# An encoder on one core: the first products in plain float32, a projection ahead of its norm's sums, and GpSimd's splits from a later point

## The chip, the cores and the metric

The kernel runs on one core of a Trainium2 chip. The time is device microseconds of one execution; three executions of the kernel before took 1354.34, 1357.28 and 1357.43 us, so their median is 1357.28 us. The engines are TensorE (PE, with its weight loads shown apart as PEld), VectorE (DVE), ScalarE (ACT), GpSimd (POOL) and SyncE (SP, which here only issues DMAs).

## The reference, cut to what matters

Input is x (1, 256, 1024) in float32, with 16 learned meta tokens prepended, so 272 tokens in all. Two layers (DEPTH = 2) run over them:

```python
def rms_norm(x, g):
    xf = x.astype(jnp.float32)
    y = xf * lax.rsqrt(jnp.mean(xf * xf, axis=-1, keepdims=True) + EPS)
    return (y * g.astype(jnp.float32)).astype(x.dtype)

def swiglu(h, w_in, w_out):
    gate, up = jnp.split(h @ w_in, 2, axis=-1)
    return (jax.nn.silu(gate) * up) @ w_out

for l in range(DEPTH):
    h = h + 0.5 * swiglu(rms_norm(h, ffn1_norm[l]), ffn1_w_in[l], ffn1_w_out[l])
    h = h + hybrid_mixer(rms_norm(h, mix_norm[l]), w_in[l], ...)
    h = h + 0.5 * swiglu(rms_norm(h, ffn2_norm[l]), ffn2_w_in[l], ffn2_w_out[l])
return rms_norm(h, final_norm)[:, META:]
```

The hidden width of the SwiGLU is 2816. The mixer makes one combined projection (q, k, v of three attentions A, B and C, and gates), runs the three attentions, multiplies each by its own output weights and its gate, adds them, and applies w_out. All inputs are float32.

## The kernel before, in words

**Layout and products.** Activations lie transposed in SBUF: `h` holds 1024 features as 8 slices of 128 partitions, each with 272 tokens (256 grid tokens, then 16 meta tokens). Every weight product is made of three TensorE products. A float32 weight block arrives by DMA as `raw` (128 x 1024, 512 KB, a "unit" of four 128-row slices and 256 columns). ACT rounds it to `hi` (L227, type float32r), and DVE or POOL writes the rest, `lo` = raw - hi (L228). The activation is split in the same way into `xh` and `xl`. `mm` then adds xh·hi, xl·hi and xh·lo in PSUM (L271, L272, L273), for each of 8 slices k and each of 2 output halves m: 48 TensorE products of 272 tokens for a 1024-deep group of 256 outputs. `raw` has 4 buffers, `hi` and `lo` have 4 each, and the PSUM tile `acc` has 2.

**The norm.** A `Norm` object keeps x' = g·h, without the factor 1/rms, as `xh` and `xl`; `pair(j)` makes two of the 8 slices (xh by DVE at L312 for the odd slice and by ACT at L314 for the even one, xl by DVE at L315), squares h on ACT (L318), and adds the squares up into `ss` (L321, on POOL, for the last pair on DVE). `finish` sums over the partitions by two plain float32 products with a matrix of ones (L326), and makes rstd `r` = 1/rms with one square root on ACT (L291, which first loads an activation table) and six DVE instructions (L329, L292 to L296). The results of the products are multiplied by r afterwards, as they leave PSUM.

**The start.** x comes in as two tiles of 128 tokens; `load_pair(j)` transposes two slices on TensorE (L191) into one PSUM bank, and ACT (L194) and DVE (L195) copy them into `h`. `norm.pair` follows. `first` holds the `hi` and `lo` of the first gate group of the first SwiGLU, and `ffn` makes its 48 products, then `finish`, then the 48 products of the first up group.

**The mixer.** `mixer` calls `norm.finish` and then makes its projections, B's values first (`B_V`, two groups of 256 outputs), then B's keys and queries, A's, C's and the gates, woven into the attentions. Each result of the first four groups is multiplied by r while it leaves PSUM (L700, L704). While `in_mixer[0]` is set, `lo_engine` gives each third unit's `lo` to POOL, by a counter that runs over all plain units of the program; the others are DVE's.

**What sets the order.** The instructions of each engine are put in their order when the kernel is built, by a scheduler that may move independent ones past each other; on the chip every engine runs its own list in order. All weight DMAs are issued by SP, in order.

Of the kernel before, what the change touches and what calls it, by code (L numbers as in the profile page):

```python
# [10 lines left out]
F32 = mybir.dt.float32  # L11
F32R = mybir.dt.float32r
AF = mybir.ActivationFunctionType
# [78 lines left out]
def encoder_kernel(ctx: ExitStack, tc: tile.TileContext, x, meta_tokens, ffn1_norm, ffn1_w_in, ffn1_w_out,  # L92
# [20 lines left out]
    def scr():  # L113
        return sb.tile([128, 2, T], F32, name=nm("scr"), tag="scr", bufs=5)

    def acc_tile():
        return ps.tile([128, 2, 512], F32, name=nm("acc"), tag="acc", bufs=2)
# [4 lines left out]
    def bc(ap, n):  # L122
        return ap[:, None, :].to_broadcast([ap.shape[0], n, ap.shape[1]])
# [61 lines left out]
    def load_pair(j):  # L185

        pt = bank("s", 3)
        for i in range(2):
            for k in range(2):
                c0 = (2 * j + k) * 128  # L190
                PE.transpose(pt[:, (2 * i + k) * 128:(2 * i + k + 1) * 128], x_nat[i][:, c0:c0 + 128], ident)  # L191
        hv = h[:, 2 * j:2 * j + 2, :GRID].rearrange("p k (c r) -> p k r c", r=ROWS)
        pv = pt.rearrange("p (i k r c) -> p i k r c", i=2, k=2, r=2)
        ACT.copy(hv[:, :, 0:2, :], pv[:, 0])  # L194
        DVE.tensor_copy(hv[:, :, 2:4, :], pv[:, 1])  # L195

    gshuf = const.tile([128, 4], F32, name="gshuf")
    swap16 = [(i + 16) % 32 for i in range(32)]
# [61 lines left out]
    def mm(acc, units, xh, xl, xk, n):  # L260

        rows = [(hi, lo, kk) for hi, lo in units for kk in range(hi.shape[1])]
        for k, (hi, lo, kk) in enumerate(rows):
            if isinstance(xh, list):
                rh, rl = xh[k // 4][:, k % 4, :n], xl[k // 4][:, k % 4, :n]
            else:
                rh, rl = xh[:, xk + k, :n], xl[:, xk + k, :n]
            for m in range(2):
                o = acc[:, m, :n]
                a, b = hi[:, kk, m * 128:(m + 1) * 128], lo[:, kk, m * 128:(m + 1) * 128]  # L270
                PE.matmul(o, a, rh, start=k == 0, stop=False)  # L271
                PE.matmul(o, a, rl, start=False, stop=False)  # L272
                PE.matmul(o, b, rh, start=False, stop=k == len(rows) - 1)  # L273
# [24 lines left out]
    class Norm:  # L298
# [5 lines left out]
            self.xl = big.tile([128, 8, T], F32R, name=nm("xl"), tag="xl")  # L304
            self.ss = big.tile([128, 2, T], F32, name=nm("ss"), tag="ss")

        def pair(self, j, n):

            for k in (2 * j + 1, 2 * j):
                g = gcol[:, self.g0 + k:self.g0 + k + 1]  # L310
                if k % 2:
                    DVE.tensor_scalar(self.xh[:, k, :n], h[:, k, :n], g, None, op0=ALU.mult)  # L312
                else:
                    ACT.activation(self.xh[:, k, :n], h[:, k, :n], AF.Copy, scale=g)  # L314
                DVE.scalar_tensor_tensor(self.xl[:, k, :n], h[:, k, :n], g, self.xh[:, k, :n].bitcast(F32),  # L315
                                         op0=ALU.mult, op1=ALU.subtract)
            dst = (scr() if j else self.ss)[:, :, :n]
            ACT.activation(dst, h[:, 2 * j:2 * j + 2, :n], AF.Square)  # L318
            if j:
                ss = self.ss[:, :, :n]  # L320
                (DVE if j == 3 else POOL).tensor_tensor(ss, ss, dst, op=ALU.add)  # L321
# [25 lines left out]
    def ffn(w1, w2, norm, nxt, n, first=None):  # L347
        r = rb = None
        for half, (k0, nk) in enumerate(((0, 12), (12, 10))):
            hh = big.tile([128, 12, T], F32R, name=nm("hh"), tag="hh")  # L350
            hl = big.tile([128, 12, T], F32R, name=nm("hl"), tag="hl")
            for j in range(nk // 2):
                ga = acc_tile()
                mm(ga, (r is None and first) or plain(w1, 0, 8, (k0 + 2 * j) * 128), norm.xh, norm.xl, 0, n)
                if r is None:
                    r = norm.finish(n)
                    rb = bc(r[:, :n], 2)
                ua = acc_tile()
                mm(ua, plain(w1, 0, 8, DFF + (k0 + 2 * j) * 128), norm.xh, norm.xl, 0, n)
                g = scr()[:, :, :n]  # L360
                gate, up = ga[:, :, :n], ua[:, :, :n]
                if half == 0 and j == 0:
                    u = scr()[:, :, :n]
                    ACT.copy(g, gate)
                    ACT.copy(u, up)
                    gate, up = g, u
                DVE.tensor_tensor(g, gate, rb, op=ALU.mult)  # L367
                ACT.activation(g, g, AF.Silu)
                DVE.tensor_tensor(g, g, rb, op=ALU.mult)
                DVE.tensor_tensor(g, up, g, op=ALU.mult)  # L370
                split(hh[:, 2 * j:2 * j + 2, :n], hl[:, 2 * j:2 * j + 2, :n], g)
            if first and not half:
                other_gains()
            for mp in range(4):
                residual(mp, plain(w2, k0 * 128, nk, mp * 256), hh, hl, n, nxt if half else None)
# [291 lines left out]
    def mixer(l, norm, nxt, last):  # L667
# [3 lines left out]
            late_dma(cst[:, n_id:], consts[:, n_id:])  # L671
            late_dma(sink, sink_a.partition_broadcast(128))
        biases = [bias_load(l, qi) for qi in range(2)]
        r = norm.finish(T)
        rb = bc(r, 2)
        xh, xl = norm.xh, norm.xl
        oh = big.tile([128, 12, T], F32R, name=nm("oh"), tag="hh")
        ol = big.tile([128, 12, T], F32R, name=nm("ol"), tag="hl")
# [6 lines left out]
        def q_tile():  # L685
            return qk(4, T)
# [4 lines left out]

        vb, kb = qk(4, 2, KB), qk(4, 2, KB)
        qb = q_tile()
        for dst, c0 in ((vb, B_V), (kb, B_K)):
            for half in range(2):
                a = proj(plain(w, 0, 8, c0 + half * 256))
                for qi in range(2):
                    t0 = qi * 96
                    for m in range(2):
                        DVE.tensor_tensor(  # L700
                            dst[:, 2 * half + m, qi, :160].rearrange("p (r c) -> p r c", r=4),
                            a[:, m, t0:t0 + 160].rearrange("p (c r) -> p r c", r=4),
                            r[:, t0:t0 + 160].rearrange("p (c r) -> p r c", r=4), op=ALU.mult)
                    DVE.tensor_tensor(dst[:, 2 * half:2 * half + 2, qi, 160:], a[:, :, GRID:T],  # L704
                                      bc(r[:, GRID:], 2), op=ALU.mult)
# [158 lines left out]
    class Final:  # L864
# [24 lines left out]
        def finish(self):  # L889
# [9 lines left out]
            for qi in range(2):  # L899
# [2 lines left out]
                ACT.activation(self.y[qi][:, 512:], self.pt[qi], AF.Copy, scale=rc)  # L902
                (nc.sync if qi == 0 else ACT).dma_start(dst[qi], self.y[qi])

    norm = Norm(0)
    load_pair(0)
    norm.pair(0, T)
    first = plain(ffn1_w_in[0], 0, 8, 0)
    for j in range(1, 4):
        load_pair(j)  # L910
        norm.pair(j, T)
    for l in range(DEPTH):
        last = l == DEPTH - 1
        nxt = Norm(16 + 8 * l)
        ffn(ffn1_w_in[l], ffn1_w_out[l], norm, nxt, T, first if l == 0 else None)
        norm, nxt = nxt, Norm(32 + 8 * l)
        in_mixer[0] = True
        mixer(l, norm, nxt, last)
        in_mixer[0] = False
        norm, nxt = nxt, (Final() if last else Norm(8))  # L920
        ffn(ffn2_w_in[l], ffn2_w_out[l], norm, nxt, GRID if last else T)
        norm = nxt
# [28 lines left out]
```

## Time and profile before

| | before |
|---|---|
| runs | 1354.34, 1357.28, 1357.43 us |
| profiled execution | 1356.25 us |
| its span, first to last instruction | 1354.5 us |
| PE busy | 1330.5 us (98%) |
| DVE busy | 888.4 us (66%) |
| ACT busy | 649.2 us (48%) |
| POOL busy | 164.7 us (12%) |
| mean granted TensorE clock | 0.991 of full |

The profile is of one execution. "Busy" is the time in which an engine had an instruction; the ends of TensorE's products are modelled and overlap, so their spacing is read from their starts. A row of the timeline gives the start, the duration, the engine, the line of the kernel, the operation, `out<-in` by the names in the program, the shape, the count, and in brackets how long the engine had been idle before it and what ended that. A plain float32 product shows as two records, a float32r product as one. Line numbers are those of the kernel before; in the changed kernel the lines from L199 on have moved (L271 to L273 are L278 to L280 there, L326 is L337, L228 is L235, L312 is L319, L315 is L322, L321 is L332).

### The profile page before, as it was taken

How to read it: one execution, taken by the hardware profiler on the slowest of the kernel's cores; microseconds unless marked ns; L12 is line 12 of the kernel's file. 1: busy time of each engine (PE TensorE's matmuls, PEld its weight loads, DVE VectorE, ACT ScalarE, POOL GpSimd, SP SyncE). 2: the span in 40 equal slices, each digit the busy share in tenths (PEclk: the TensorE clock that was granted, in tenths of full speed). 3: DMA queues.
4: the chain of work that ended last, by engine and by line, in shares of the span. 5: the costliest groups of instructions: out<-in, count | busy, mean ns of one | idle time of the engine just before them, and what ended most of it. 6: DMA issues, size and time to landing. Idle time of an engine off the chain costs nothing.

```text
span 1354.5 us, 25919 instructions
## 1 busy us (share of the span) xinstructions
PE 1330.5 (98%) x10699; PEld 1290.3 (95%) x10699; DVE 888.4 (66%) x1319; ACT 649.2 (48%) x933; POOL 164.7 (12%) x99
## 2 busy tenths in 40 slices
PE   8999999999999999999999999999999999999997
PEld 7999999988898999999999999999889899999997
DVE  7655668588555587646676556676876556865663
ACT  6443444466454455434455434445555545544444
POOL 1000002332122210000000000022322233000000
PEclk9999999999999999999999999999989999999998
DMA  7765556432334566555565555454324456665652
GB/s 218 203 184 176 181 177 188 141 109 89 115 110 125 176 195 187 184 172 173 162 187 180 171 175 182 158 172 149 101 86 118 133 154 192 192 188 187 187 172 78
DMA packets 239010, 217.52 MB, mean 161 GB/s; under 512 B 24804, under 2 KB 237980, under 8 KB 238764
## 3 DMA queue, kind: packets, MB, share of 16 engines
q1 hardware_dynamic: 238540, 215.20, 52.0%
q8 instruction: 84, 1.38, 0.4%
q10 hardware_dynamic: 352, 0.66, 0.1%
q14 instruction: 34, 0.28, 0.1%
HBM read 214.78 MB, written 1.05 MB: 159 GB/s over the span
## 4 chain that ended last, share of the span: by engine, by line
PE 92%; DVE 5%; ACT 1%; issue 1%; DMA 0%; SPq 0%; DVEq 0%; ACTq 0%
PE acc L272 28%; PE acc L271 28%; PE acc L273 28%; PE s L465 2%; PE pv L423 2%; DVE lo L228 1%; PE s L488 1%; PE s L627 1%; PE s L639 1%; ACT hi L227 1%; PE pv L418 1%; DMA raw<-in_ffn_w_in_dram 0%; PE s L326 0%; DVE xl L315 0%; DVE p L408 0%
## 5 line engine op out<-in xcount | busy, mean ns | idle before, releaser
L227 ACT CAST hi<-raw 128x1024 fp32r<-128x1024 f32 (+1 forms) x392 | 404.5, 1033 | 572.0 <-PE acc L272 403.0
L272 PE MATMUL acc<-xl,hi 128*128 128x272 f32 (+1 forms) x2176 | 629.0, 289 | 1.9 <-DVE xl L315 1.8
L271 PE MATMUL acc<-xh,hi 128*128 128x272 f32 (+1 forms) x2176 | 626.3, 288 | 1.0 <-ACT xh L314 1.0
L273 PE MATMUL acc<-xh,lo 128*128 128x272 f32 (+1 forms) x2176 | 625.5, 288 | 0.7 <-DVE lo L228 0.7
L228 DVE TENSOR_TENSOR lo<-raw,hi 128x1024 fp32r<-128x1024 f32 (+1 forms) x352 | 428.4, 1218 | 215.5 <-ACT hi L227 215.1
L271 PEld LDWEIGHTS acc<-xh,hi 128*128 128x128 f32 x2176 | 412.7, 190 | 11.1 <-issue 7.4
L272 PEld LDWEIGHTS acc<-xl,hi 128*128 128x128 f32 x2176 | 411.5, 189 | 5.9 <-issue 2.9
L273 PEld LDWEIGHTS acc<-xh,lo 128*128 128x128 f32 x2176 | 411.6, 189 | 3.5 <-issue 2.3
L272 PE MATMUL acc<-hl,hi 128*128 128x272 f32 (+1 forms) x704 | 201.8, 287 | 0.0
L273 PE MATMUL acc<-hh,lo 128*128 128x272 f32 (+1 forms) x704 | 201.1, 286 | 0.0
L271 PE MATMUL acc<-hh,hi 128*128 128x272 f32 (+1 forms) x704 | 200.4, 285 | 0.0
L271 PEld LDWEIGHTS acc<-hh,hi 128*128 128x128 f32 x704 | 132.7, 189 | 0.1
L273 PEld LDWEIGHTS acc<-hh,lo 128*128 128x128 f32 x704 | 132.3, 188 | 0.0
L272 PEld LDWEIGHTS acc<-hl,hi 128*128 128x128 f32 x704 | 132.2, 188 | 0.0
L228 POOL TENSOR_TENSOR lo<-raw,hi 128x1024 fp32r<-128x1024 f32 x40 | 97.3, 2434 | 286.1 <-ACT hi L227 274.1
L321 POOL TENSOR_TENSOR ss<-ss,scr 128x544 f32<-128x544 f32 (+1 forms) x12 | 17.5, 1459 | 601.1 <-ACT scr L318 601.1
L271 PE MATMUL acc<-oh,hi 128*128 128x272 f32 (+1 forms) x192 | 54.7, 285 | 0.0
L272 PE MATMUL acc<-ol,hi 128*128 128x272 f32 (+1 forms) x192 | 54.6, 284 | 0.0
L273 PE MATMUL acc<-oh,lo 128*128 128x272 f32 (+1 forms) x192 | 54.4, 283 | 0.0
L370 DVE TENSOR_TENSOR scr<-acc,scr 128x544 f32<-128x544 f32 (+1 forms) x40 | 28.7, 717 | 31.5 <-PE acc L273 31.4
L280 DVE SCALAR_TENSOR_TENSOR h<-acc,h 128x544 f32<-128x544 f32 (+1 forms) x40 | 28.5, 714 | 28.6 <-PE acc L273 28.5
L367 DVE TENSOR_TENSOR scr<-acc,rstd 128x544 f32<-128x544 f32 (+1 forms) x40 | 28.6, 716 | 26.2 <-PE acc L273 26.2
(234 smaller groups left out, 1296.8 us busy)
## 6 DMA issues: line engine op xcount, KB each, us to landing
raw<-in_ffn_w_in_dram SPq DMA_DIRECT2D x176, 512.0 KB, 3.6
raw<-in_ffn_w_out_dram SPq DMA_DIRECT2D x80, 512.0 KB, 3.4
raw<-in_w_in_dram SPq DMA_DIRECT2D x80, 512.0 KB, 3.7
raw<-in_w_in_dram SPq DMA_DIRECT2D x32, 256.0 KB, 3.3
raw<-in_w_branch_dram SPq DMA_DIRECT2D x32, 256.0 KB, 3.8
raw<-in_w_out_dram SPq DMA_DIRECT2D x16, 512.0 KB, 3.4
raw<-in_ffn_w_out_dram SPq DMA_DIRECT2D x16, 256.0 KB, 2.7
raw<-in_w_branch_dram SPq DMA_DIRECT2D x8, 512.0 KB, 3.5
```

The costliest lines, as they stand in the source:

```text
L227: ACT.copy(hi[:, :n], raw[:, :n])
L228: lo_engine().tensor_tensor(lo[:, :n], raw[:, :n], hi[:, :n].bitcast(F32), op=ALU.subtract)
L271: PE.matmul(o, a, rh, start=k == 0, stop=False)
L272: PE.matmul(o, a, rl, start=False, stop=False)
L273: PE.matmul(o, b, rh, start=False, stop=k == len(rows) - 1)
L280: DVE.scalar_tensor_tensor(hv, a[:, :, :n], 0.5, hv, op0=ALU.mult, op1=ALU.add)
L321: (DVE if j == 3 else POOL).tensor_tensor(ss, ss, dst, op=ALU.add)
L367: DVE.tensor_tensor(g, gate, rb, op=ALU.mult)
L370: DVE.tensor_tensor(g, up, g, op=ALU.mult)
L418: PE.matmul(pv[:, t * 128:(t + 1) * 128], vm[:, t * 128:(t + 1) * 128], pmt, start=t == 0, stop=False)
L423: PE.matmul(pv[g * HD:(g + 1) * HD, t * 128:(t + 1) * 128], a, b, start=vm is None and kt == 0, stop=kt == 1 and (vm is None or t == 3))
L465: PE.matmul(s, q[g * HD:(g + 1) * HD, t, qi * 128:(qi + 1) * 128], kk[g * HD:(g + 1) * HD, :], start=True, stop=True)
```

## The change

Three things change.

**First group.** The first gate group of the program is made by 16 plain float32 products, of the unrounded weights in `raw` with x' itself, kept in a new tile `x32`, which shares its place with the later `hh`. x' is written straight from the PSUM bank of the transposes (ACT for even slices, DVE for odd ones, with the gain as scale); `h` is copied from the same bank later. All four pairs are loaded before the first `norm.pair`, and this norm's split is made of two slices at a time, by one ACT copy and one DVE subtraction. The two weight units of this group are not split and not counted by `lo_engine`.

**Mixer.** The first projection of each mixer (first half of `B_V`) is placed ahead of `norm.finish`. Its result is copied from PSUM by ACT into a scratch tile of SBUF (L707 of the changed kernel), and multiplied by r from there.

**GpSimd.** `in_mixer[0]` is set from B's keys on, not from the start of the mixer, so B's values have no `lo` on POOL. With the two units that are no longer counted, the counter also stands elsewhere when it reaches the mixers: counted from 0 over the 60 plain units of a mixer, POOL had units 0, 3, 6, ... in the first mixer and 2, 5, 8, ... in the second; now it has 5, 8, 11, ... in the first and 4, 7, 10, ... in the second.

```diff
@@ load_pair
-        hv = h[:, 2 * j:2 * j + 2, :GRID].rearrange("p k (c r) -> p k r c", r=ROWS)
-        pv = pt.rearrange("p (i k r c) -> p i k r c", i=2, k=2, r=2)
-        ACT.copy(hv[:, :, 0:2, :], pv[:, 0])
-        DVE.tensor_copy(hv[:, :, 2:4, :], pv[:, 1])
+        hv = h[:, 2 * j:2 * j + 2, :GRID].rearrange("p k (c r) -> p k c r", r=ROWS)
+        pv = pt.rearrange("p (i k r c) -> p k c i r", i=2, k=2, r=2)
+        for k in range(2):
+            g = gcol[:, 2 * j + k:2 * j + k + 1]
+            xv = x32[:, 2 * j + k, :GRID].rearrange("p (c i r) -> p c i r", i=2, r=2)
+            if k:
+                DVE.tensor_scalar(xv, pv[:, k], g, None, op0=ALU.mult)
+            else:
+                ACT.activation(xv, pv[:, k], AF.Copy, scale=g)
+        for i in range(2):
+            (DVE.tensor_copy if i else ACT.copy)(hv[:, :, :, 2 * i:2 * i + 2], pv[:, :, :, i])
@@ Norm.pair
+            if whole is not None:
+                k = slice(2 * j, 2 * j + 2)
+                ACT.copy(self.xh[:, k, :n], whole[:, k, :n])
+                DVE.tensor_tensor(self.xl[:, k, :n], whole[:, k, :n], self.xh[:, k, :n].bitcast(F32), op=ALU.subtract)
@@ ffn
-                ga = acc_tile()
-                mm(ga, (r is None and first) or plain(w1, 0, 8, (k0 + 2 * j) * 128), norm.xh, norm.xl, 0, n)
+                if r is None and first is not None:
+                    ga = first
+                else:
+                    ga = acc_tile()
+                    mm(ga, plain(w1, 0, 8, (k0 + 2 * j) * 128), norm.xh, norm.xl, 0, n)
@@ mixer
-        r = norm.finish(T)
-        rb = bc(r, 2)
...
+        a = scr()
+        ACT.copy(a, proj(plain(w, 0, 8, B_V))[:, :, :T])
+        r = norm.finish(T)
+        rb = bc(r, 2)
         for dst, c0 in ((vb, B_V), (kb, B_K)):
+            in_mixer[0] = dst is kb
             for half in range(2):
-                a = proj(plain(w, 0, 8, c0 + half * 256))
+                if half or dst is kb:
+                    a = proj(plain(w, 0, 8, c0 + half * 256))
@@ the start
     norm = Norm(0)
-    load_pair(0)
-    norm.pair(0, T)
-    first = plain(ffn1_w_in[0], 0, 8, 0)
-    for j in range(1, 4):
+    x32 = big.tile([128, 12, T], F32, name="x32", tag="hh")
+    DVE.tensor_tensor(x32[:, :8, GRID:], h[:, :, GRID:], gcol[:, :8, None].to_broadcast([128, 8, META]), op=ALU.mult)
+    first = acc_tile()
+    raws = []
+    for i in range(2):
+        raw = wts.tile([128, 1024], F32, name=nm("raw"), tag="raw", bufs=RAW)
+        nc.sync.dma_start(raw.rearrange("p (k c) -> p k c", k=4),
+                          ffn1_w_in[0][i * 512:(i + 1) * 512, :256].rearrange("(k p) c -> p k c", p=128))
+        raws.append(raw)
+    for j in range(4):
         load_pair(j)
-        norm.pair(j, T)
+        for k in (2 * j, 2 * j + 1):
+            for m in range(2):
+                c0 = (k % 4) * 256 + m * 128
+                PE.matmul(first[:, m, :T], raws[k // 4][:, c0:c0 + 128], x32[:, k, :], start=k == 0, stop=k == 7)
+    for j in range(4):
+        norm.pair(j, T, x32)
```

How the instructions stand on their engines, at the three places where most of it moves:

TensorE at the start of the program, before: `s_167` is the bank of the last transposes, `acc_186` the first gate group.

```order
L191 MATMUL s_167<-cst,p_90 128x128 x2
L191 MATMUL s_167<-cst,p_91 128x128 x2
L271 MATMUL acc_186<-xh_112,hi_128 128x272
L272 MATMUL acc_186<-xl_113,hi_128 128x272
L273 MATMUL acc_186<-xh_112,lo_129 128x272
```

The same place in the changed kernel: `acc_117` is the first gate group, `acc_209` the first up group, `x_115` the tile `x32`, `s_161` the bank of the last transposes.

```order
L939 MATMUL acc_117<-x_115,raw_118 128x272 x8
L939 MATMUL acc_117<-x_115,raw_120 128x272 x4
L191 MATMUL s_161<-cst,p_90 128x128 x2
L191 MATMUL s_161<-cst,p_91 128x128 x2
L278 MATMUL acc_209<-xh_112,hi_211 128x272
L279 MATMUL acc_209<-xl_113,hi_211 128x272
L280 MATMUL acc_209<-xh_112,lo_212 128x272
L939 MATMUL acc_117<-x_115,raw_120 128x272 x2
```

Twelve of the sixteen plain products now stand ahead of the last transposes, and the first split products behind them belong to the up group; the last slice's two plain products follow five split products later.

ACT at the start of the changed kernel, from its first casts on: `raw_210` and `raw_216` are the two units of the up group.

```order
L329 ACTIVATE ss_114<-h 128x544
L326 CAST xh_112<-x_115 128x544
L329 ACTIVATE scr_179<-h 128x544
L326 CAST xh_112<-x_115 128x544
L329 ACTIVATE scr_184<-h 128x544
L234 CAST hi_211<-raw_210 128x1024
L234 CAST hi_217<-raw_216 128x1024
L200 ACTIVATE x_115<-s_161,gcol 128x256
```

Ahead of these rows stand three writes of `x_115`, three copies into `h` and one more cast of `xh`; so the first `hi` of the up group comes behind twelve ACT instructions. Before, the first `hi` (of the gate group) stood behind two.

VectorE at the entry of the first mixer, before: `h` is the last residual of the SwiGLU, `ss_183` the norm's sum of squares.

```order
L228 TENSOR_TENSOR lo_2402<-raw_2400,hi_2401 128x1024
L228 TENSOR_TENSOR lo_2463<-raw_2461,hi_2462 128x1024
L280 SCALAR_TENSOR_TENSOR h<-acc_2265,h 128x544
L312 TENSOR_SCALAR xh_181<-h,gcol 128x272
L315 SCALAR_TENSOR_TENSOR xl_182<-h,gcol,xh_181 128x272 x2
L321 TENSOR_TENSOR ss_183<-ss_183,scr_2331 128x544
L228 TENSOR_TENSOR lo_2530<-raw_2528,hi_2529 128x1024
L329 TENSOR_SCALAR scr_2381<-s_2377 128x272
```

And now:

```order
L235 TENSOR_TENSOR lo_2353<-raw_2351,hi_2352 128x1024
L235 TENSOR_TENSOR lo_2427<-raw_2425,hi_2426 128x1024
L287 SCALAR_TENSOR_TENSOR h<-acc_2227,h 128x544
L235 TENSOR_TENSOR lo_2433<-raw_2431,hi_2432 128x1024
L319 TENSOR_SCALAR xh_192<-h,gcol 128x272
L322 SCALAR_TENSOR_TENSOR xl_193<-h,gcol,xh_192 128x272 x2
L332 TENSOR_TENSOR ss_194<-ss_194,scr_2293 128x544
L235 TENSOR_TENSOR lo_2494<-raw_2492,hi_2493 128x1024
L340 TENSOR_SCALAR scr_2411<-s_2407 128x272
```

One more `lo` (2433, formerly POOL's) stands between the residual and the norm's last pair. On TensorE the two products of `finish` stood behind 27 of the first projection's 48 products, and in the second mixer behind 31; now they stand behind all 48 in both. On ACT a `hi`, the copy of the first projection and then the load of the square root's table stand, in this order, between the norm's last square and the square root.

More of the change, by code (lines that the diff above doesn't have):

```diff
@@ L305, in __init__, with pair @@
             self.ss = big.tile([128, 2, T], F32, name=nm("ss"), tag="ss")
-        def pair(self, j, n):
-            for k in (2 * j + 1, 2 * j):
+        def pair(self, j, n, whole=None):
+            for k in (2 * j + 1, 2 * j) if whole is None else ():
                 g = gcol[:, self.g0 + k:self.g0 + k + 1]
@@ L371, in ffn @@
                 split(hh[:, 2 * j:2 * j + 2, :n], hl[:, 2 * j:2 * j + 2, :n], g)
-            if first and not half:
+            if first is not None and not half:
                 other_gains()
@@ L916, in encoder_kernel @@
         norm, nxt = nxt, Norm(32 + 8 * l)
-        in_mixer[0] = True
         mixer(l, norm, nxt, last)
```

## The prediction

> **What bounds the kernel now.** I read the page first, then the chain of waits, then TensorE's own waits, and last the timeline at the places where those lie.
>
> ```profile
> span 1354.5 us, 25919 instructions
> PE 1330.5 (98%) x10699; PEld 1290.3 (95%) x10699; DVE 888.4 (66%) x1319; ACT 649.2 (48%) x933; POOL 164.7 (12%) x99
> PE 92%; DVE 5%; ACT 1%; issue 1%; DMA 0%; SPq 0%; DVEq 0%; ACTq 0%
> ```
>
> TensorE sets the time nearly everywhere: it holds 92% of the chain. An edit pays only where it lets TensorE start sooner, wait less, or do less. TensorE's waits (us in total, times, longest):
>
> ```profile
> PE s L326 <- DVE ss L321: 2.8, 2, 1.9
> PE acc L798 <- ACT scr L794: 2.3, 1, 2.3
> PE acc L272 <- DVE xl L315: 1.8, 2, 1.6
> ```
>
> The first row is the entry of the two mixers; the last is the start, where smaller ones stand beside it. The change aims at both places. The start in the timeline:
>
> ```profile
> 7.51 1.08 ACT L194 COPY h<-s 128x256 f32<-128x256 f32 x2 [4.09 <-PE s L191]
> 8.83 0.66 PE L191 MATMUL s<-cst,p 128*128 128x128 f32 x4 [0.49 <-DVE h L195]
> 8.96 1.05 ACT L227 CAST hi<-raw 128x1024 fp32r<-128x1024 f32 x1 [0.36 <-DMA raw<-in_ffn_w_in_dram]
> 10.47 0.39 PE L271 MATMUL acc<-xh,hi 128*128 128x272 f32 x1 [0.98 <-ACT xh L314]
> 18.96 0.40 PE L272 MATMUL acc<-xl,hi 128*128 128x272 f32 x1 [1.56 <-DVE xl L315]
> 22.09 1.08 PE L326 MATMUL s<-ss,ones 128*128 128x272 f32 x4
> 22.81 0.49 PE L271 MATMUL acc<-xh,hi 128*128 128x272 f32 x1
> 23.14 0.28 PE L272 MATMUL acc<-xl,hi 128*128 128x272 f32 x1
> 28.63 0.28 PE L271 MATMUL acc<-xh,hi 128*128 128x272 f32 x1
> ```
>
> The first weights land at 8.96, products begin at 10.47, and the second gate group begins at 28.63. Between 23.14 and 28.63 lie 44 split products without a wait, 0.125 us each. So the 96 products of the first two groups (12.0) and the sum (0.92, below) would fill 12.9 of the 18.16 us from 10.47 on; 5.2 are waits and a slow clock.
>
> **The start, worked out.** *Removed:* 48 split products, 6.0 us, and two `hi` and two `lo`. *Added:* 16 plain float32 products of 272 tokens. Their price is in the rows above: from 22.09 to 23.14 TensorE took two of them and one split product, so (1.05 - 0.125)/2 = 0.46 us each; by the starts alone, (22.81 - 22.09)/2 = 0.36. I take 0.46, as the next product's start at 23.14 shows that the second was still going: 16 x 0.46 = 7.36, that is 1.4 us more work than before. The gain must come from what needs no split: the products need only the landed weights and x'.
>
> What the up group needs comes later now, behind twelve ACT instructions. Their prices:
>
> ```profile
> L286 ACT CAST hh<-scr 128x544 fp32r<-128x544 f32 x33 | 21.2, 642 | 0.6 <-DVE scr L370 0.6
> L318 ACT ACTIVATE scr<-h 128x544 f32<-128x544 f32 x15 | 9.6, 642 | 0.0
> L228 DVE TENSOR_TENSOR lo<-raw,hi 128x1024 fp32r<-128x1024 f32 x336 | 417.4, 1243 | 198.8 <-ACT hi L227 198.3
> L321 POOL TENSOR_TENSOR ss<-ss,scr 128x544 f32<-128x544 f32 x10 | 14.5, 1454 | 597.8 <-ACT scr L318 597.8
> L287 DVE TENSOR_TENSOR hl<-scr,hh 128x544 fp32r<-128x544 f32 x33 | 23.7, 719 | 0.0
> ```
>
> ACT starts at 7.51 as before: three writes of x' and three copies at 0.54 (half of the row at 7.51), three casts and three squares at 0.64, together 7.08; then `hi` 1.05: ready at 15.64, its `lo` on DVE at 16.88. TensorE: twelve plain products from 8.96 end at 14.48, four transposes (0.66) at 15.14, two split products at 15.39; then it waits 1.5 for that `lo`. Two plain products and five split ones bring it to 18.56; the last slice of x' (DVE, behind the second `lo`) is there at 16.88 + 1.24 + 0.54 = 18.66: wait 0.1. Two plain and fifteen split products end at 21.47; the norm's sum needs a `lo`, a copy, an `xl` and the add on DVE: 18.66 + 1.24 + 0.54 + 0.72 + 0.71 = 21.87: wait 0.4. The sum (0.92) and 25 products (3.12) end at 25.9. Against 28.63 that is **2.7 us gained**. Without any of these waits it would be 4.7. The other end: POOL's adds of squares may hold DVE up (below) by one add, 1.45, and a window of half clock may fall into it, 1.7; together -0.5. SP issues the first four weight DMAs in the same order as before; the fifth now waits for eight plain products, until 12.6, and ACT needs it only near 17. x32 is read for the last time near 20, and `hh` in its place is written after r, so that costs nothing.
>
> **The mixers, worked out.**
>
> ```profile
> 215.07 0.28 PE L271 MATMUL acc<-xh,hi 128*128 128x272 f32 x1
> 220.51 1.18 PE L326 MATMUL s<-ss,ones 128*128 128x272 f32 x4 [1.91 <-DVE ss L321]
> 892.50 0.28 PE L271 MATMUL acc<-xh,hi 128*128 128x272 f32 x1
> 897.47 1.18 PE L326 MATMUL s<-ss,ones 128*128 128x272 f32 x4 [0.94 <-DVE ss L321]
> 216.32 2.39 POOL L228 TENSOR_TENSOR lo<-raw,hi 128x1024 fp32r<-128x1024 f32 x1 [3.42 <-ACT hi L227]
> 216.68 2.19 DVE L312 TENSOR_SCALAR xh<-h,gcol 128x272 fp32r<-128x272 f32 x1
> 885.94 0.36 DVE L312 TENSOR_SCALAR xh<-h,gcol 128x272 fp32r<-128x272 f32 x1
> 219.74 0.72 DVE L321 TENSOR_TENSOR ss<-ss,scr 128x544 f32<-128x544 f32 x1
> ```
>
> The sum waits for `ss` while 21 and 17 ready products stand behind it. With all 48 ahead, TensorE reaches the sum at 215.07 + 6.0 = 221.1 and 892.50 + 6.0 = 898.5, after `ss` of before was done (220.46, and shortly before 897.47). The rows also show why `ss` was late: the same DVE instruction takes 0.36 us alone and 2.19 under POOL's split, ending as that ends. Without that split and with one more `lo` on DVE, `ss` moves by -1.83 + 1.24, to 219.9. Both waits go: **2.85 us gained**. The other end is 0.9, if the wait moves to the last pair's xl (needed at 215.07 + 36 x 0.125 = 219.6; 219.2 by the same sum, 219.8 if a POOL instruction still holds it).
>
> What is late next is r. ACT's table load used to run during the wait; now a `hi`, the copy and the load precede the root.
>
> ```profile
> 219.26 1.28 ACT L291 ACT_TABLE_LOAD   x1
> 222.21 0.43 ACT L291 ACTIVATE rstd<-scr 128x272 f32<-128x272 f32 x1 [1.67 <-DVE scr L329]
> L364 ACT COPY scr<-acc 128x544 f32<-128x544 f32 x3 | 1.8, 606 | 0.0
> 222.67 1.85 DVE L292 RECIPROCAL rstd<-rstd 128x272 f32<-128x272 f32 x1 [0.50 <-ACT rstd L291]
> 228.26 0.78 DVE L700 TENSOR_TENSOR qk<-acc,rstd 128x160 f32<-128x160 f32 x2
> ```
>
> From 221.07: `hi` 1.05, copy 0.61 (L364 is its like), load 1.28, root 0.43: 224.4; reciprocal 1.85, a `lo` 1.24, four short ones of 0.44: r at 229.3 instead of 228.26; two evacuations of 1.65 each (four like L700's and two shorter ones): 232.6. The fourth projection needs the second's PSUM tile at 221.07 + 0.92 + 12.0 = 234.0. So 1.4 us of cover are left, and the lateness costs nothing. The copy itself, one per mixer, lies on an ACT that is 48% busy.
>
> **Sum.** 2.7 + 2.85 = 5.5 us off a span of 1354.5; the profiled execution took 1356.25, 1.75 more than its span, and the median of the runs shown is 1.03 above that. I take it off the median: 1357.28 - 5.5 = **1351.8 us**.
>
> **Rivals.**
>
> *The evacuation is held up by POOL.* The first six evacuations in each mixer now read SBUF twice where they read PSUM and SBUF.
>
> ```profile
> 901.52 0.44 DVE L293 TENSOR_TENSOR scr<-rstd 128x272 f32<-128x272 f32 x1
> 901.87 2.40 POOL L228 TENSOR_TENSOR lo<-raw,hi 128x1024 fp32r<-128x1024 f32 x1 [7.21 <-ACT hi L227]
> 902.00 2.57 DVE L294 TENSOR_TENSOR scr<-scr 128x272 f32<-128x272 f32 x1
> ```
>
> An instruction with both inputs in SBUF took 2.57 beside a POOL split where its neighbour took 0.44; L700, with one input in PSUM, took 0.78 for two at 228.26, under the POOL split of 228.40. One hold of 2.4 uses the 1.4 of cover and costs 1.0 per mixer: 1353.8. Against it: by the order of ACT the splits near that place start at 222 and 232. The Trainium skill (SBUF — State Buffer, "Who interferes with whom") says that such a DVE instruction contends with a GpSimd one that reads SBUF, and that whichever comes second fully blocks; the trace agrees.
>
> *Half clock in the plain products.*
>
> ```profile
> 12.10:15.50 3.40, 3.12 (x12) 2.80 (x13) 3.40 (x4) 3.40 (x6) 1.49 (x1) 0.52 0.73 216
> 319.30:322.70 3.40, 2.50 (x17) 2.15 (x18) 3.40 (x9) 1.19 (x4) 1.33 (x1) 1.00 0.80 247
> 322.70:326.10 3.40, 3.40 (x19) 3.13 (x18) 2.94 (x11) 0.61 (x2) 0.00 (x0) 0.52 0.01 2
> 995.10:1005.40 10.30, 10.30 (x45) 9.37 (x45) 6.53 (x24) 5.37 (x13) 1.33 (x1) 0.51 0.20 60
> ```
>
> (us, then busy time of PE, PEld, DVE, ACT, POOL, then the granted clock.) The clock halves for stretches of 3.4 us, or three of them, behind a wait of TensorE. If two such stretches cover the plain products, they cost 3.4 and the start gains nothing: 1355.2. Against it: TensorE is busy from 8.96 on. The skill (TensorE: Matmul & The Clock Gate, "What's actually happening") has the clock fall after an idle window of about 3.4 us, with windows that run free of the kernel; by that rule the wait of 1.5 is too short.
>
> *POOL's turns fall better.* The second mixer's wait of 2.3 (L798) and the half clock behind it (10.3 us, 5.2 lost) come after a POOL split that held DVE. The second mixer now has turns that no trace shows; if these two go, 5.5 + 7.5: 1344.3.
>
> *Slower: POOL's turns fall worse.* The place is the same, C's queries in each mixer. The first mixer takes over about the second's turns, so it may get the longer stretch too (6.9 us more at half clock, 3.5 lost). From 11 us of added half clock over both mixers the gain is gone; with 20 us, two stretches of 10 more, it is 1357.28 - 5.5 + 10 = 1361.8. For it: both mixers had a stretch there. Against it: the total before was 13.7.
>
> **How the numbers follow.** Forecast 0.55 (1349.7 with both terms at their better ends, 1356.9 at their worse ones), evacuation held 0.12, half clock at the start 0.12, better turns 0.15, worse turns 0.06. A measurement of this kernel tells 0.3%, 4.1 us, from no change: below 1353.2 is faster. Of the forecast about nine tenths lie there (0.48), all of the better turns, and a third of the two small rivals, less 0.04 for what I left out: 0.67. Slower is 0.06, same 0.27. The range of 8 in 10 takes in both small rivals and most of the better turns: 1345.5 to 1355.5.
>
> **What would show it.** At the start: plain products from about 9.0, 0.46 apart; TensorE waiting once more than 1 us, for DVE's `lo`; the second gate group beginning near 25.9 instead of 28.6; no half clock before 20. At the mixers: no wait of L337 for `ss`, L319 at 0.36, r about 1 us later after the sum, no wait of the fourth projection. I am wrong if the second gate group begins after 27.5, if a new wait stands in the first 20 us of a mixer, or if waits and half clock at C's queries change by more than 3 us.

## The result, and the profile after

| | before | changed |
|---|---|---|
| runs of the first comparison, us | 1354.34 to 1357.60, median 1357.28 | 1346.27 to 1349.73, median 1349.38 |
| changed / before | | 0.9945, 95% interval 0.9934 to 0.9957 |
| the same in a second comparison (below) | | 0.9954, 0.9939 to 0.9969 |
| span of the profiled execution, us | 1354.5 | 1344.5 |
| mean granted clock of it | 0.991 | 0.994 |

The kernel became faster by 7.5 us in the first comparison and by 6.2 in the second (each ratio applied to 1355). I had forecast 5.5. That is just outside the first interval (5.8 to 8.9 us) and inside the second (4.2 to 8.3). One execution of a kernel further below, the one with the paired query units' `lo` on DVE, took 2596.46 us, and it is in none of the ratios.

The page of the changed kernel, its span, busy times and the shares of the chain of waits:

```profile
span 1344.5 us, 25887 instructions
PE 1326.9 (99%) x10683; PEld 1286.6 (96%) x10683; DVE 890.4 (66%) x1316; ACT 649.5 (48%) x937; POOL 159.5 (12%) x97
PE 93%; DVE 5%; ACT 1%; issue 1%; DMA 0%; ACTq 0%; DVEq 0%
```

TensorE's waits there (us in total, times, longest):

```profile
PE s L479 <- DVE sm L402: 3.4, 4, 1.3
...
PE acc L280 <- DVE lo L235: 0.7, 1, 0.7
...
PE acc L278 <- DVE qk L722: 0.6, 1, 0.6
```

The waits for `ss` (2.8) and for `scr` at C's queries (2.3) are gone. What is left at the entries is 0.6, a new wait for an evacuation, that is, for the DVE instructions that read a finished projection and so free its place in PSUM. At C's queries the waits for `sm` (L479, formerly L465) have grown from 2.5 to 3.4; before, the row was

```profile
PE s L465 <- DVE sm L388: 2.5, 3, 1.7
```

The start in the timeline:

```profile
9.00 5.74 PE L939 MATMUL acc<-x,raw 128*128 128x272 f32 x24 [0.76 <-DMA raw<-in_ffn_w_in_dram]
11.85 3.13 POOL L332 TENSOR_TENSOR ss<-ss,scr 128x544 f32<-128x544 f32 x2 [10.63 <-ACT scr L329]
12.17 0.69 ACT L329 ACTIVATE scr<-h 128x544 f32<-128x544 f32 x1
12.73 2.01 ACT L234 CAST hi<-raw 128x1024 fp32r<-128x1024 f32 x2
13.83 3.38 DVE L235 TENSOR_TENSOR lo<-raw,hi 128x1024 fp32r<-128x1024 f32 x2
16.12 0.39 PE L280 MATMUL acc<-xh,lo 128*128 128x272 f32 x1 [0.69 <-DVE lo L235]
20.76 1.16 PE L337 MATMUL s<-ss,ones 128*128 128x272 f32 x4
24.88 0.28 PE L278 MATMUL acc<-xh,hi 128*128 128x272 f32 x1
```

The last row is the beginning of the second gate group: 24.88, where it was 28.63. The start gained 3.75 us, not 2.7. All of it is still there at the first product of the first mixer, which begins at 211.32 instead of 215.07.

The gain does not simply add up from there. Two later points of the program stand at the same work in both kernels: the sum of the norm behind the first mixer and that of the norm behind the second. The kernel before reaches them at

```profile
500.50 1.08 PE L326 MATMUL s<-ss,ones 128*128 128x272 f32 x4
...
1161.85 1.03 PE L326 MATMUL s<-ss,ones 128*128 128x256 f32 x4
```

and the changed kernel at

```profile
497.52 1.08 PE L337 MATMUL s<-ss,ones 128*128 128x272 f32 x4
...
1151.86 1.03 PE L337 MATMUL s<-ss,ones 128*128 128x256 f32 x4
```

So behind the first mixer only 2.98 us are left of the start's 3.75 and of the entry's gain, and behind the second mixer 9.99. In between, in each mixer, lie C's queries, where the half clock is: 3.4 us before and 6.8 after in the first mixer, 10.2 before and none after in the second. The experiments had to tell how much of the result is the two terms of my sum and how much is this.

### The profile page after: what moved, and what is told of

Its sections match the earlier page's. It is cut to its first block, busy times and chain, and to the rows that moved or that the text cites. A ratio compares the mean times of both kernels' runs of the same rounds, so it can differ in the third digit from the quotient of the medians.

```text
span 1344.5 us, 25887 instructions
## 1 busy us (share of the span) xinstructions
PE 1326.9 (99%) x10683; PEld 1286.6 (96%) x10683; DVE 890.4 (66%) x1316; ACT 649.5 (48%) x937; POOL 159.5 (12%) x97
## 4 chain that ended last, share of the span: by engine, by line
PE 93%; DVE 5%; ACT 1%; issue 1%; DMA 0%; ACTq 0%; DVEq 0%
PE acc L279 29%; PE acc L280 28%; PE acc L278 28%; PE s L479 2%; PE pv L437 2%; PE s L502 1%; DVE lo L235 1%; PE s L641 1%; PE pv L432 1%; DVE p L422 1%; PE s L653 1%; PE s L337 0%; DMA qk<-in_meta_tokens_dram 0%; DVE p L402 0%; ACT hi L234 0%
## 5 line engine op out<-in xcount | busy, mean ns | idle before, releaser
L279 PE MATMUL acc<-xl,hi 128*128 128x272 f32 (+1 forms) x2160 | 622.5, 288 | 0.0
L278 PE MATMUL acc<-xh,hi 128*128 128x272 f32 (+1 forms) x2160 | 619.9, 287 | 0.6 <-DVE qk L722 0.6
L278 PEld LDWEIGHTS acc<-xh,hi 128*128 128x128 f32 x2160 | 408.2, 189 | 9.6 <-issue 7.1
L279 PEld LDWEIGHTS acc<-xl,hi 128*128 128x128 f32 x2160 | 406.9, 188 | 4.5 <-issue 4.1
L280 PEld LDWEIGHTS acc<-xh,lo 128*128 128x128 f32 x2160 | 407.0, 188 | 3.7 <-issue 2.5
L235 POOL TENSOR_TENSOR lo<-raw,hi 128x1024 fp32r<-128x1024 f32 x38 | 92.4, 2432 | 256.5 <-ACT hi L234 243.3
```

What stands on the lines that cost most here:

```text
L235: lo_engine().tensor_tensor(lo[:, :n], raw[:, :n], hi[:, :n].bitcast(F32), op=ALU.subtract)
```

## The experiments

Ratios are to the kernel before, run on the same chip in the same session, with their 95% intervals; "us" behind a ratio is that ratio applied to 1355.

### Each part alone

The start alone: the changed start, with the mixers and POOL's turns as before.

```diff
-    unit_no = [0]
+    unit_no = [2]
+    x32 = big.tile([128, 12, T], F32, name="x32", tag="hh")
...
+        norm.pair(j, T, x32)
```

> The plain float32 start alone; the mixers and POOL's turns are as before. Theory (the start's gain is TensorE's own and is kept): the second gate group begins at 24.9 us instead of 28.6, all later milestones lie 3.7 us earlier, and the time is 3.7 us below the kernel before; both waits for ss at the mixers' entries (1.9 and 0.9) and the half clock at C's queries of the second mixer stay. Rival (the start shifts which stretches run at half clock, or the next wait eats it): the second gate group begins early all the same, but the time falls by less than 2 us.

Measured: 0.9984 (0.9974 to 0.9993), 2.2 us. The second gate group began at 24.61, so the local gain is there. The interval, 0.9 to 3.5 us, ends just below the 3.7 expected. Part of it was given back: the waits for `ss` at the mixers grew from 2.8 to 3.4 us. Where the rest went is not shown.

```profile
PE s L337 <- DVE ss L332: 3.4, 2, 2.5
```

The entry alone: the first projection ahead of the norm's sums, POOL's splits from the start of the mixer as before.

```diff
-        r = norm.finish(T)
-        rb = bc(r, 2)
...
+        a = scr()
+        ACT.copy(a, proj(plain(w, 0, 8, B_V))[:, :, :T])
+        r = norm.finish(T)
+        rb = bc(r, 2)
```

> The first projection of each mixer ahead of its norm's sums, alone; start, GpSimd splits and turns as before, so POOL still holds DVE in the entry. Theory (order is what counts): both waits for ss go, 2.85 us less TensorE waiting, time 2.9 us below the kernel before. Rival (POOL's hold on DVE is what counts): the wait moves from ss to the last pair's xl, some 0.3 to 1.9 us of it stays at the first mixer's entry, and the time falls by 1 to 2 us.

Measured: 0.9966 (0.9954 to 0.9978), 4.6 us. No wait for `ss` or for the last pair's `xl` is left, although POOL still held DVE's L312 for 2.18 us (216.43); a wait of 0.6 for the evacuation has come. The first theory holds for the waits: the order alone covers the hold. The time fell by more than the theory's 2.9, which lies just outside the interval (3.0 to 6.2 us); where the rest comes from is open.

```profile
216.43 2.18 DVE L312 TENSOR_SCALAR xh<-h,gcol 128x272 fp32r<-128x272 f32 x1
...
PE acc L271 <- DVE qk L707: 0.6, 1, 0.6
```

GpSimd's later begin alone:

```diff
-        in_mixer[0] = True
         mixer(l, norm, nxt, last)
...
         for dst, c0 in ((vb, B_V), (kb, B_K)):
+            in_mixer[0] = dst is kb
```

> GpSimd splits from B's keys on, alone; start as before, and the first projection still behind the norm's sums as before. Theory (order is what counts): DVE's L312 at the first mixer's entry falls from 2.19 to 0.36 us, but one more lo on DVE takes 1.24 back, so the wait for ss there falls by only 0.6 to 0.9 and the time by 0.5 to 1.5. Rival (POOL's hold on DVE is what counts): both waits for ss go, and the time falls by 2.9 us.

Measured: 0.9985 (0.9974 to 0.9995), 2.0 us. L312 fell to 0.35 as expected, but both waits for `ss` were gone, so my expectation for the entry failed. The reason is in the order: with the `lo` on DVE, the scheduler put the sum behind 35 products of the first projection, instead of 27 in the first mixer and 31 in the second. This edit therefore moves the sum too, and does not separate the order from the hold.

### The same wait removed twice?

Two of the three parts remove the same wait. If one is enough, the earlier projection could be taken back.

```diff
-        a = scr()
-        ACT.copy(a, proj(plain(w, 0, 8, B_V))[:, :, :T])
         r = norm.finish(T)
...
-                if half or dst is kb:
-                    a = proj(plain(w, 0, 8, c0 + half * 256))
+                a = proj(plain(w, 0, 8, c0 + half * 256))
```

> The changed kernel without its second part: the first projection of each mixer stands behind the norm's sums again, and is read from PSUM; the start and GpSimd's later begin stay. Theory (the later begin and the earlier projection remove the same wait, one is enough): no wait for ss above 0.3 us at either entry, the wait of 0.64 us for L722's evacuation in the second mixer is gone, and the time is that of the changed kernel or up to 1 us below it. Rival (the earlier projection carries the entry's gain): waits for ss of 1 to 2 us are back, and the time is 2 to 3 us above the changed kernel.

Measured: 0.9998 (0.9983 to 1.0014): all of the change's gain is gone. The rival is right that the earlier projection is needed, but the loss, 6 to 7 us against the two comparisons of the changed kernel, is more than its 2 to 3. TensorE's waits at the two entries:

```profile
PE s L598 <- DVE qk L715: 1.6, 2, 1.0
...
PE s L337 <- DVE ss L332: 1.2, 1, 1.2
```

That is 2.8 us where the changed kernel has 0.6: 2.1 us. The wait for `ss` stands in the first mixer (217.25). POOL held two `xl` ahead of it, by the add of squares this time, not by a split:

```profile
209.34 1.38 POOL L332 TENSOR_TENSOR ss<-ss,scr 128x544 f32<-128x544 f32 x1 [9.14 <-ACT scr L329]
209.41 2.02 DVE L322 SCALAR_TENSOR_TENSOR xl<-h,gcol,xh 128x272 fp32r<-128x272 f32 x2
```

(0.91 for two without POOL.) This hold alone does not make the wait: it stands in the changed kernel as well (208.90, 2.03 us) and in the run with GpSimd's later begin alone (212.00, 2.04 us), and neither waits for `ss`.

The waits do not explain all of the 6 to 7 us. The runs of this kernel went from 1348.86 us at a mean clock of 0.996 to 1359.09 at 0.988, so their spread is half clock. On average over its runs, (1 - clock) x span is 11.6 us, against 8.9 and 9.7 in the changed kernel's two comparisons: that is 2 to 3 us more lost to the clock. The rest, and why this order draws more half clock, I did not settle.

The opposite kernel, with the earlier projection and the new start but GpSimd's splits from the start of the mixer, was not run. So what the later begin is worth beside the earlier projection is not shown.

### GpSimd's turns at C's queries

The change also gave POOL other turns. These two kernels start the counter of units elsewhere, and so try the other two of the three possible turns; the first has those of the kernel before.

```diff
-    unit_no = [0]
+    unit_no = [2]
```

The second kernel has `[1]` in its place.

> The changed kernel, with the counter of GpSimd's turns started at 2, so that POOL has units 0, 3, 6, ... of the first mixer and 2, 5, 8, ... of the second from B's keys on, as before. Theory (what the change gained at C's queries of the second mixer comes from the other turns): the wait of about 2.3 us there and some 10 us of half clock behind it are back, half clock in the first mixer is 3.4 us instead of 6.8, and the time is 2 to 4 us above the changed kernel. Rival (turns do not matter, the stretches of half clock come by chance or by the earlier arrival): the time is within 0.7 us of the changed kernel.

> The changed kernel with the third of the possible turns of GpSimd: the counter starts at 1. Theory (the turns decide which waits stand at C's queries, and with them the half clock): the waits there are others than with the counter at 0 or 2, and the time differs from the changed kernel by 2 us or more, up or down. Rival (the turns only move the holds about): the waits differ, the time is within 1.5 us of the changed kernel.

Measured: 0.9937 (0.9920 to 0.9954) and 0.9957 (0.9943 to 0.9971); the changed kernel has 0.9945. The three cannot be told apart. The first kernel's trace did what the theory said, and the time did not: the wait of 2.3 us is back behind a held DVE instruction, with 6.8 us of half clock behind it,

```profile
978.33 3.13 POOL L235 TENSOR_TENSOR lo<-raw,hi 128x1024 fp32r<-128x1024 f32 x1 [0.20 <-ACT hi L234]
979.13 2.41 DVE L492 TENSOR_TENSOR pm<-p,sm 128x64 f32<-128x64 f32 x1
987.71 1.87 PE L816 MATMUL acc<-cst,scr 128*128 128x2 f32 x8 [2.28 <-ACT scr L812]
```

(L492 takes 0.21 alone, as at 987.99 in the same trace), while other waits are gone. The other two turns have a hold in the second mixer as well. In the changed kernel it is this one, with the wait for `sm` behind it (L804 took 0.42 in the kernel before, as L786 at 977.58):

```profile
972.31 2.36 POOL L235 TENSOR_TENSOR lo<-raw,hi 128x1024 fp32r<-128x1024 f32 x1 [5.00 <-ACT hi L234]
972.57 2.40 DVE L804 TENSOR_TENSOR k<-k,scr 128x272 f32<-128x272 f32 x1
975.44 0.72 PE L479 MATMUL s<-k,qk 64*128 64x272 f32 x2 [1.23 <-DVE sm L402]
```

With `[1]`, L788 took 2.85 us at 989.83 under a split, and a wait of 2.17 for `sm` ended at 993.89. So in these three kernels the turn chose which instruction was held, not whether one was.

### No split on GpSimd

If it is the hold that costs, it should go with the splits.

```diff
-            in_mixer[0] = dst is kb
+            in_mixer[0] = False
```

> The changed kernel with every lo of the plain units on DVE, none on GpSimd. Theory (at C's queries TensorE waits because a GpSimd split holds one DVE instruction for 2.2 us, more than the 1.24 us that the lo costs on DVE): no DVE instruction of 0.2 to 0.4 us takes over 2 there, the waits for sm and scr at C's queries fall by about 1 us each, fewer stretches of half clock follow, and the time is 2 to 5 us below the changed kernel. Rival (DVE has no room for 1.24 us more per third unit): the waits for DVE in the mixers grow, and the time is 3 us or more above the changed kernel.

Measured: 0.9882 (0.9868 to 0.9896), 16.0 us below the kernel before and some 9 below the changed kernel: more than the theory's 2 to 5. In its trace TensorE waits neither for `sm` at L479 nor for `scr` at L816, and there is no half clock from the first product to the end. DVE, with 23.7 us more work (914.1 busy), had room. All four times lie within 1.3 us. That POOL's splits are slow in themselves is not what costs: in none of the traces does TensorE wait for a `lo` of POOL. The edit also changes the order of DVE's list, and no run separates that from the hold.

The same edit on the kernel before (`in_mixer[0] = False` in the place of `True`):

> The kernel before with one edit: every lo of the plain units on DVE, none on GpSimd. Theory (GpSimd's hold on DVE is behind both the waits for ss at the entries and the waits at C's queries): L312 takes 0.36 us at both entries and the waits for ss fall below 1 us each, the wait of 2.3 us for scr and that of 1.7 us for sm at C's queries go and with them the half clock there (13.7 us in the profile before), and the time is 7 to 11 us below the kernel before. Rival (the changed kernel's other parts are needed for this): it gains less than 4 us.

Measured: 0.9926 (0.9913 to 0.9940), 10.0 us. This one edit, of one word, is worth more than the whole change; all five times (1344.60 to 1345.14) lie below the eleven of the changed kernel. Both waits for `ss` are gone here as well (the sum again stands behind 35 products); TensorE waits at the entries for the evacuation instead, and C's queries of the second mixer run without half clock (columns: stretch; its length, then busy time of PE, PEld, DVE, ACT, POOL; granted clock; DMA share; GB/s):

```profile
PE s L584 <- DVE qk L700: 1.9, 2, 1.0
```

```profile
972.00:995.00 23.00, 22.98 (x167) 19.77 (x167) 20.66 (x69) 16.84 (x37) 2.62 (x2) 1.00 0.15 47
```

With the hold gone, the earlier projection was taken back once more:

```diff
-            in_mixer[0] = dst is kb
+            in_mixer[0] = False
...
-        a = scr()
-        ACT.copy(a, proj(plain(w, 0, 8, B_V))[:, :, :T])
         r = norm.finish(T)
```

> The changed kernel with no plain lo on GpSimd, and with the first projection of each mixer behind the norm's sums again. Theory (with the hold gone the earlier projection has little left to win): waits for ss and L715's evacuation of 1 to 2 us in all, time 0.5 to 2 us above the same kernel with the earlier projection (1338.7). Rival (the earlier projection is worth what it seemed to be beside GpSimd's splits): 4 to 7 us above it.

Measured: 0.9910 (0.9894 to 0.9926), 1341.56 us against 1338.68 with the earlier projection: 2.9 us by the medians, on two chips, and 3.8 by the ratios; both lie between theory and rival. Against the kernel before without splits, on the same chip, the start is worth 3.2 us by the medians (1344.76 to 1341.56) and 2.2 by the ratios. The two readings differ because one of the five times of this kernel is 1345.98 and the other four are 1341.12 to 1342.63. So without POOL's splits the start is worth 2.2 to 3.2 (2.7 forecast) and the entries 2.9 to 3.8 (2.85 forecast); their sum, 6.0 to 6.1, is firmer than its parts.

Two further steps in the same direction: first the paired query units' `lo` all on DVE, then the adds of squares too.

```diff
-                (DVE if g else POOL).tensor_tensor(lv[:, :, :, g], ...)
+                DVE.tensor_tensor(lv[:, :, :, g], ...)
```

> The changed kernel with no lo on GpSimd at all, also not the half lo of the paired query units (L232, sixteen of 1.28 us). Theory (any GpSimd split costs DVE more than it saves): DVE's own half of 1.3 us falls to 0.7, and the waits that are left for DVE in the mixers stay or fall, time 0 to 2 us below the kernel with no plain lo on GpSimd. Rival (DVE is full there): 1 us or more above it.

```diff
-                (DVE if j == 3 else POOL).tensor_tensor(ss, ss, dst, op=ALU.add)
+                DVE.tensor_tensor(ss, ss, dst, op=ALU.add)
```

> The changed kernel with no lo at all on GpSimd, and the adds of squares (L332) on DVE too, so that GpSimd holds DVE at no start, no norm and no projection. Theory (in the start the two adds held DVE's two lo's for 1.0 us: 3.4 instead of 2.35): the lo's take 1.2 each, the wait for lo near 15 us stays below 1.0, the second gate group begins no later than 24.9, and the time is 0 to 1 us below the kernel that only has no lo on GpSimd (1337.3). Rival (twelve adds of 0.7 us more on DVE come in front of what TensorE waits for): a wait for ss or lo of 1 us or more appears at the start or at a norm, and the time is 1 to 3 us above that kernel.

Measured: 0.9869 (0.9853 to 0.9884) and 0.9857 (0.9844 to 0.9870), the latter 1336.19 to 1336.60 us in all its runs. Each step is small beside its interval; together with the first one they give the fastest kernel of this study, 19 us below the kernel before and 13 below the changed one, which had 0.9954 in the same session. In its start the two `lo` take 2.36 instead of 3.38, and the wait for them is gone; a wait of 0.46 for `ss` has come:

```profile
13.65 2.36 DVE L235 TENSOR_TENSOR lo<-raw,hi 128x1024 fp32r<-128x1024 f32 x2
...
20.57 1.15 PE L337 MATMUL s<-ss,ones 128*128 128x272 f32 x4 [0.46 <-DVE ss L332]
```

### The changed kernel once more

> The changed kernel once more, as it is, beside the next one on the same chip. Theory (at C's queries its waits of 0.7 to 1.3 us are near the point from which half clock follows, so the number of 3.4 us stretches differs from run to run): times spread over 3 us or more, the longer ones at the lower mean clock, and the middle within 0.25% of 0.9945 of the kernel before. Rival (the spread of the first five runs was an accident): all within 1.5 us.

Measured: 0.9954 (0.9939 to 0.9969), 1347.05 us at a mean clock of 0.995 to 1352.77 at 0.992. The theory holds, and two profiles of one kernel show how. In the first, TensorE waits 1.23 us for `sm` at 975.44, in the second 1.24 at 975.02. The rows are stretches of 3.41 us on the grid on which the half clock begins and ends, and in the last row of the second profile four of them. First profile, then second:

```profile
971.18:974.59 3.41, 3.03 (x21) 2.34 (x19) 3.41 (x7) 2.33 (x2) 2.28 (x1) 1.00 0.00 0
974.59:978.00 3.41, 2.56 (x14) 1.64 (x14) 3.21 (x13) 2.35 (x10) 0.08 (x1) 1.00 0.50 154
978.00:988.24 10.24, 10.24 (x78) 9.14 (x78) 9.08 (x28) 6.87 (x16) 1.79 (x2) 1.00 0.16 43
```

```profile
971.80:975.22 3.42, 2.19 (x13) 1.50 (x12) 3.42 (x6) 1.51 (x3) 2.36 (x1) 1.00 0.00 0
975.22:988.87 13.65, 13.65 (x51) 10.86 (x51) 8.10 (x31) 5.91 (x19) 1.27 (x1) 0.50 0.13 40
```

In the first the edge of the grid cuts the wait (0.38 of it in one stretch, 0.85 in the next) and nothing follows. In the second the whole wait lies in one stretch and 13.65 us of half clock follow, 6.8 us lost. The edges do not stand at the same place of the program in the two profiles, and here one and the same wait cost 1.2 us in one and 8 in the other. That the cut made the difference is read from this one pair.

## Why the prediction was right, point by point

**The start: right in kind, mis-sized.** Plain products came at 9.00, twelve of them in 5.57 us: 0.464 each, the 0.46 I took. No half clock before 20. The failed step is "ready at 15.64" for `hi`: I added up the durations of ACT's twelve instructions, 7.08 us, but they took 5.32 (7.41 to 12.73), because each begins before the recorded end of the last. The six casts and squares began 0.53 to 0.56 apart although they last 0.65 to 0.69 (12.17 to 12.73, for one), which makes 0.6 of the difference; the three copies took 0.80 where I had 1.62, and the three writes of x' 1.24 where I had 1.62. So ACT reached `hi` at 12.73, not 14.59. The trace of the kernel before shows such spacings too: a square of 0.64 at 10.33, the next instruction at 10.88. Against that, POOL's adds did hold DVE: two `lo` took 3.38 where 2.35 is their own time, the other end that I had named. So the wait for `lo` was 0.69 instead of 1.5, those of 0.1 and 0.4 behind it did not come, and the second gate group began at 24.88 instead of 25.9. I called a group after 27.5 wrong; in the nine other profiles with this start it began between 24.53 and 26.04, and in the four with the old start between 28.38 and 28.82. Those four all have one or two stretches of half clock in the first 19 us, and none of the ten with the new start has.

**The entries: right.** No wait for `ss`, as forecast, L319 at 0.35:

```profile
214.89 0.35 DVE L319 TENSOR_SCALAR xh<-h,gcol 128x272 fp32r<-128x272 f32 x1
...
217.32 1.08 PE L337 MATMUL s<-ss,ones 128*128 128x272 f32 x4
...
225.38 0.80 DVE L718 TENSOR_TENSOR qk<-scr,rstd 128x160 f32<-128x160 f32 x2
```

From the sum to the first use of r (L718) it is 8.06 us, 8.2 by my sum. My reason was incomplete, though: that a split held L312 explains the late `ss`, but the wait also goes with that hold left in place (the entry alone), and 0.9 us of it stood in the first mixer of the kernel with no split on POOL and the projection behind the sums. In every trace with the whole projection ahead of the sum, no wait for `ss` stands at the entries.

**The evacuation held by POOL: it came, in one mixer of two.**

```profile
903.58 3.03 DVE L718 TENSOR_TENSOR qk<-scr,rstd 128x160 f32<-128x160 f32 x2
903.68 2.61 POOL L235 TENSOR_TENSOR lo<-raw,hi 128x1024 fp32r<-128x1024 f32 x1 [7.50 <-ACT hi L234]
909.24 0.36 PE L278 MATMUL acc<-xh,hi 128*128 128x272 f32 x1 [0.64 <-DVE qk L722]
```

The two evacuations took 3.03 instead of 0.80, and TensorE waited 0.64, where I had priced one hold at 1.0. The wait is that of the fourth projection, for which I had forecast none, and it ends 19.7 us behind the mixer's first product (889.52). So this was one of my own signs of being wrong: a new wait in the first 20 us of a mixer. The step that failed is the place of the splits: I had argued against the hold from where they stand in ACT's order; in the first mixer that was right (splits at 218.56 and 228.48, none between), in the second wrong. The Trainium skill (SBUF — State Buffer, "Who interferes with whom") has the later of the two block until the first is done; the trace agrees, with 2.2 us lost to a split of 2.61.

**C's queries: here too I was wrong by my own test.** Half clock at C's queries changed from 13.65 to 6.83 us in the profiles, more than the 3 us that I allowed, and the wait of 2.3 us for `scr` went. But the cause that I gave this case (better turns) fell: with the old turns the wait is back and the time is not. What stands behind it in the second mixer is POOL's hold, which all three turns have, and, as far as one pair of profiles shows, the phase of the grid. So the part of the profiles' 10.0 us that came from C's queries was luck: in the changed kernel's second profile the half clock there is more than before, 17.1 us against 13.65. Without the splits the change is worth 6.1 us (1344.76 to 1338.68, on two chips; 6.0 by the ratios), 5.5 forecast; 6.1 lies within the intervals of both comparisons (7.5 and 6.2 us).

**The rivals that did not come:** half clock in the plain products was in none of the profiles with this start, and no worse turn was found.

## What to carry to other kernels

A GpSimd instruction that reads SBUF can be paid by VectorE: here a split of 2.4 us on GpSimd held a 0.2 us instruction for 2.2, more than the 1.24 that VectorE needs to do the split itself. Before work is balanced onto an engine that seems free, look in the timeline for short instructions that take its length and end with it, and try the kernel without it. And where two edits remove the same wait, try each without the other on the chip: here, without the one that looked spare, none of the gain was left. When a start is added up, take the spacing of an engine's starts from the trace, not the durations.

## What the runs showed of the hardware that was not expected

**A short wait can be followed by far more half clock than its own length, or by none.** Half clock began and ended on a grid of 3.41 us and lasted one to four of its stretches. In thirteen profiles (all but the one of the next paragraph), every stretch at full clock in which weight loads (PEld) were busy less than 1.3 us was followed by half clock (11 of 11); of the twelve between 1.3 and 1.6 us, four were, and three more were followed with 1.72 to 2.35 us. The busy time of TensorE alone does not order them: this stretch of the changed kernel, with PE busy for 2.67 us, was followed by 6.8 us of half clock, while the one with 2.56 above was not.

```profile
312.41:315.82 3.41, 2.67 (x15) 1.56 (x13) 3.41 (x11) 2.41 (x5) 0.68 (x1) 1.00 0.30 77
315.82:322.65 6.83, 6.83 (x33) 6.56 (x34) 5.04 (x14) 0.62 (x2) 0.66 (x1) 0.50 0.11 38
```

In four profiles half clock near 260 came behind a stretch without a wait (PE busy throughout, weight loads 2.47 to 2.64 us); that is open. The Trainium skill (TensorE: Matmul & The Clock Gate, "What's actually happening") has windows of 3.41 us that run free of the kernel, and the slow state after at least one idle window. The grid agrees. For the idle window the measurement decides: here windows that were idle for 0.7 to 2.3 of 3.41 us were followed by half clock.

**A granted clock of 0.95 cost nothing that shows.** The profile of the changed kernel without splits shows this clock for 883 us on end:

```profile
6.90:889.80 882.90, 879.54 (x6973) 856.66 (x6973) 602.77 (x850) 422.00 (x585) 38.32 (x30) 0.95 0.55 168
889.80:1331.27 441.47, 438.22 (x3687) 422.22 (x3685) 309.98 (x500) 225.66 (x351) 28.10 (x22) 1.00 0.50 152
```

Yet the 199.0 us between the sums of two norms (493.63 to 692.65) are the same as at full clock in the changed kernel (497.52 to 696.52), and its time lies beside those of the other runs (1339.41 against 1338.16 to 1339.12, which had 0.997).
